# One encoder layer on one core: the launch, with its loads, first rounding and products on zeros in another order

## The chip, the cores and the metric

The kernel runs on 1 core of one Trainium2 chip. A core has five engines that run side by side, each with its own queue of instructions: TensorE (PE, matrix products, with its weight loads shown as PEld), VectorE (DVE), ScalarE (ACT), GpSimd (POOL) and SyncE (SP, which here only issues DMAs). The metric is the device time of one execution in microseconds (us). The median of 3 runs of the kernel before is 2184.84 us (2183.32 to 2185.92).

## What is computed

The reference is one encoder layer on x of 512 tokens by 2048 features, in float32:

```python
h = rmsnorm(x, attn_norm_w[l])
proj = h @ w_in[l]
...
attn = mixture_of_dilations(_heads(aq, ATTN_HEADS), _heads(ak, ATTN_HEADS),
                            _heads(av, ATTN_HEADS), rel_bias_table)
...
mixed = jnp.concatenate([attn_out, gla_out], axis=-1) @ w_out[l]
x = x + mixed

h = rmsnorm(x, ffn_norm_w[l])
x = x + (jax.nn.silu(h @ w_gate[l]) * (h @ w_up[l])) @ w_down[l]
...
return rmsnorm(x, final_norm_w)
```

Only the first two lines matter for this change: the launch prepares h, and the first products compute the columns of proj that hold the attention values.

## The kernel before

**Products.** TensorE multiplies in a rounded float type (fp32r). To keep float32 accuracy, every operand is held as two tiles: hi, the value rounded to fp32r, and lo, the rest (value minus hi). A product is then three matmuls that add into one PSUM bank: hi by hi, hi by lo, lo by hi. In run_job these are lines 346 to 348, in the order x-hi by weight-hi, x-hi by weight-lo, x-lo by weight-hi.

**Weights.** The class Stream (object st) loads weights in pieces of 512 KB (two k blocks of 128 rows by 512 columns). A piece has two halves, and half n is the weights of loop step n of a job. load() issues the DMAs on SP while fewer than st.limit pieces are held. split(upto) rounds halves up to that number: ACT casts hi (L237), and rests() has DVE subtract to get lo (L218).

**x.** xt holds x as loaded, tokens on partitions. prep(k) makes feature block k of h: four transposes on TensorE against the identity tile idn (L450) put the block into a PSUM bank; ACT scales it by the norm weight column wcol into hi (L455); for k < 2 DVE computes lo straight from PSUM (L457), and ACT then writes the unrounded block into fB (L458); for k of 2 and more DVE takes lo from that unrounded block (L460). ACT and DVE take turns on one PSUM bank. Each pair of blocks q (2q and 2q+1) is followed by sums_x(q), a generator of three steps: sums of quarter blocks on DVE, then two steps that round them (L154 on ACT, L145 on DVE). It waits in the deque side, and run_side lets it advance by about one step at the end of each loop step.

**The launch.** The kernel begins with a memset of the tile warm to zero, then idn is loaded on SP's queue and wrow1 (the norm weights) on ACT's. start0, which the first job calls, makes five products of warm by warm (spin(5), two instructions each), then issues on SP, alternately, four x blocks of 256 KB (first_x, L423) and four weight blocks of 256 KB (L1127): x block 0, weight half 0, x block 1, weight half 1 and so on, and after them the rest of x, two further weight pieces and small tensors. It then transposes wrow1 into wcol, calls prep(0), makes three products on zeros and rounds the first weight half.

**The first job.** job_av(0) has 16 loop steps, one for each k. In step i four banks b = 0 to 3 get three matmuls each. The function between0(i, b), called ahead of bank b, places the next blocks of h: prep(1) ahead of bank 2 of step 0, prep(2) and prep(3) in step 1, and prep(i+2) ahead of bank 2 of each later step. before0(i) adds the sums of squares on ACT (L498) from step 3 on. The second weight half is rounded at the start of step 1.

**Order.** The program is scheduled by hand: each engine executes its instructions in the order of the Python code, and waits on semaphores for what it reads or overwrites. Slots hands out tile buffers first in, first out.

Of the kernel before, what the change touches and what calls it, by code (L numbers as in the profile page):

```python
# [19 lines left out]
OP = mybir.AluOpType  # L20
# [92 lines left out]
def put(*slots):  # L113
    for s in slots:
        if s.home is not None:
            s.home.free.append(s.i)


def layer(nc, tc, x, attn_norm_w, w_in, rel_table, gw_f, gb_f, gw_b, gb_b, gla_norm_w, w_out,
# [3 lines left out]
    w_gate, w_up, w_down, out = w_gate[0], w_up[0], w_down[0], out[0]  # L123
    pe, act, dve, pool, sp = nc.tensor, nc.scalar, nc.vector, nc.gpsimd, nc.sync
    mm = pe.matmul

    with tc.manual_schedule(), \
# [6 lines left out]
        s4 = Slots(p4, N4, 1024, "b")  # L134
# [24 lines left out]
        idn = cst.tile([P, P], F32, name="idn")  # L159
# [83 lines left out]
        st = Stream()  # L243
        AHEAD = 3
# [16 lines left out]
        side = deque()  # L261
# [46 lines left out]
        def run_job(j):  # L308
            if j.start:
                j.start()  # L310
            if j.limit:
                st.limit = j.limit
            banks = j.banks or [ps.get() for _ in range(4)]
            per = len(j.kts) // j.n
            for i in range(j.n):
                if j.before and j.tail is None:
                    j.before(i)
                st.load()
                st.split(j.first + i + (min(AHEAD, i + 1) if j.between else j.lead(i)) +
                         (0 if j.tail is None else max(0, 4 * (4 * j.tail + i - 3) // 3)))  # L320
                if j.tail is not None:
                    j.before(i)
                st.lag = j.fine
                st.rests(j.first + i + 1)
                _, _, wh, wl = st.halves[j.first + i]
                ks = j.kts[i * per:(i + 1) * per]
                for b in range(4):
                    if j.between:
                        j.between(i, b)
                    for s_, k in enumerate(ks):  # L330
                        xh, xl = j.acts(k)
                        first = i == 0 and s_ == 0
                        last = i == j.n - 1 and s_ == per - 1
                        if j.kind == "A":
                            o = banks[b].t
                            c = slice(b * P, (b + 1) * P)
                            mm(o, wh.t[:, c], xh.t, start=first, stop=False)  # L337
                            mm(o, wh.t[:, c], xl.t, start=False, stop=False)  # L338
                            mm(o, wl.t[:, c], xh.t, start=False, stop=last)  # L339
                        else:  # L340
                            n = 512 // per
                            o = banks[b].t[:, 0:n]
                            c = slice(b * P, (b + 1) * P)
                            w = slice(s_ * n, (s_ + 1) * n)
                            on = bool(j.banks)
                            mm(o, xh.t[:, c], wh.t[:, w], start=first and not on, stop=False, skip_group_check=on)  # L346
                            mm(o, xh.t[:, c], wl.t[:, w], start=False, stop=False, skip_group_check=on)  # L347
                            mm(o, xl.t[:, c], wh.t[:, w], start=False, stop=last, skip_group_check=on)  # L348
                    if j.fine and b < 3:
                        state["credit"] += j.rate / 4  # L350
                        if state["credit"] >= 1:
                            state["credit"] -= 1
                            run_side(1)
                put(wh, wl)
                if j.drop:
                    for k in ks:
                        j.drop(k)
                state["ahead"] += j.ahead
                while state["ahead"] >= 1:
                    state["ahead"] -= 1  # L360
                    next(state["sums"], None)
                if i < j.n - 1:
                    state["credit"] += j.rate / 4 if j.fine else j.rate
                    n = int(state["credit"])
                    state["credit"] -= n
                    run_side(n)
            j.evac(banks)
# [62 lines left out]

        dve.memset(warm, 0.0)
        xt[0] = [s4.get(F32, [P, 4, 256]) for _ in range(2)]
        sp.dma_start(out=idn, in_=c_idn)
        act.dma_start(out=wrow1, in_=attn_norm_w[0].rearrange("(r c) -> r c", c=P))

        rb = {}
        hT = {}
# [6 lines left out]
        def prep(k):  # L444

            w = wcol[:, W_ATT + k:W_ATT + k + 1]
            q, odd = divmod(k, 2)
            b = ps.get()
            for t in range(4):
                pe.transpose(b.t[:, t * P:(t + 1) * P], x_block(k, t), idn)  # L450
            hi, lo = hT[k] = s4.pair()
            if not odd:
                fB[q] = s4.get(F32, [P, 2, 512])
            f = fB[q].t[:, odd]
            act.activation(hi.t, b.t, AF.Copy, scale=w)  # L455
            if k < 2:
                dve.scalar_tensor_tensor(lo.t, b.t, w, hi.f, op0=OP.mult, op1=OP.subtract)  # L457
            act.activation(f, b.t, AF.Copy, scale=w)  # L458
            if k >= 2:
                dve.tensor_tensor(lo.t, f, hi.f, op=OP.subtract)  # L460
            put(b)
            if odd:
                side.append(sums_x(q))

        def block_sums(f, t13, t24):

# [7 lines left out]
        def sums_x(q):  # L474

            a, z = slice(0, 256), slice(256, 512)
            f = fB.pop(q)
            t_ = s4.get(F32, [P, 2, 512])
            t13, t24 = t_.t[:, 0], t_.t[:, 1]
            block_sums(f.t, t13, t24)  # L480
            put(f)
            yield
            x_ = {}
            slots, (x_["T2"], x_["T4"]) = side_by_side(t24, KEEP_X)
            yield
            more, (x_["T1"], x_["T3"]) = side_by_side(t13, KEEP_X)
            put(t_)
            for name, k, h in (("B11", 2 * q, a), ("B21", 2 * q + 1, a), ("B22", 2 * q + 1, z)):
                x_[name] = hT[k][0].whole[:, :, h]
            xi[q] = dict(x_, slots=slots + more)  # L490
            yield
# [617 lines left out]
        def spin(n):  # L1109

            b = ps.get()
            for _ in range(n):
                mm(b.t[:, 0:P], warm, warm, start=True, stop=True)
            put(b)

        def start0():
            tables(EXP_LN)
            spin(5)
            for k in range(4):
                first_x(k)  # L1120
                if k % 2 == 0:
                    pc = st.pieces[k // 2]
                    pc[1] = s4.get()
                    st.held += 1
                    st.n_dma += 1
                for src, dst in pc[0]:
                    sp.dma_start(out=dst(pc[1].t)[:, k % 2:k % 2 + 1], in_=src[:, k % 2:k % 2 + 1])  # L1127
            for c in range(1, 4):
                xt[c] = [s2.get() for _ in range(4)]
            load_x(1, 0, 256)  # L1130
            st.limit = 3
            st.load()
            load_x(1, 256, 512)
            st.limit = 4
            st.load()
            load_x(2, 0, 512)
            load_x(3, 0, 512)
            for r, w in ((0, ffn_norm_w), (16, gla_norm_w), (24, gb_f), (28, gb_b)):
                n = w[0].shape[0] // P
                sp.dma_start(out=wrow2[r:r + n], in_=w[0].rearrange("(r c) -> r c", c=P))  # L1140
            bias_loads(sp)
            b = ps.get(F32, [P, 16])
            pe.transpose(b.t, wrow1, idn[0:16, 0:16])
            dve.tensor_copy(wcol[:, 0:16], b.t)
            put(b)
            prep(0)
            spin(3)
            st.split(1)

        def between0(i, b):  # L1150
            if i == 0 and b == 2:
                prep(1)
            if i == 1 and b in (1, 3):
                prep(2 + b // 2)
            if i > 1 and b == 2 and i + 2 < KT:
                prep(i + 2)
# [179 lines left out]
        for c in range(4):  # L1336
            j = job("B", [piece512(w_out, c * 512, k) for k in range(0, KT, 2)], list(range(KT)),
                    lambda k: mixh[k], evac_out(c), rate=1.0, start=start_out(c), before=before_out(c), limit=3)
# [654 lines left out]
        for c in range(4):  # L1993
            j = job("B", [piece512(w_down, c * 512, k) for k in (0, 2)], list(range(4)),
                    lambda k: gT[k], evac_down(c), before=before_down(c))
# [153 lines left out]
```

## Time and profile before

| what | value |
|---|---|
| median of 3 runs | 2184.84 us |
| the profiled execution, span | 2184.5 us |
| PE busy | 2163.5 us |
| DVE busy | 1770.9 us |
| ACT busy | 1195.3 us |
| PE busy in the first 17 us | 12.74 us |
| PE busy from 17 to 100 us | 83.00 us |

The times are from one profiled execution. In a line of the order of time the first number is the start in us, the second the duration; then come engine, source line, operation, output tile, input tiles, shapes, and in square brackets the idle time just before and what ended it. "b" and "a" are the two families of buffers (4 KB and 2 KB for each partition), "ps" a PSUM bank. SPq and ACTq are DMAs issued on the queue of that engine. In a line of waits, the first engine and line waited for the second: total us, times, longest us. Matmuls are pipelined, so the start of the next one tells more than the duration of one.

### The profile page before, as it was taken

How to read it: one execution, taken by the hardware profiler on the slowest of the kernel's cores; microseconds unless marked ns; L12 is line 12 of the kernel's file. 1: busy time of each engine (PE TensorE's matmuls, PEld its weight loads, DVE VectorE, ACT ScalarE, POOL GpSimd, SP SyncE). 2: the span in 40 equal slices, each digit the busy share in tenths (PEclk: the TensorE clock that was granted, in tenths of full speed). 3: DMA queues.
4: the chain of work that ended last, by engine and by line, in shares of the span. 5: the costliest groups of instructions: out<-in, count | busy, mean ns of one | idle time of the engine just before them, and what ended most of it. 6: DMA issues, size and time to landing. Idle time of an engine off the chain costs nothing.

```text
span 2184.5 us, 34570 instructions
## 1 busy us (share of the span) xinstructions
PE 2163.5 (99%) x12618; PEld 1904.8 (87%) x12618; DVE 1770.9 (81%) x3072; ACT 1195.3 (55%) x2190; POOL 338.8 (16%) x474
## 2 busy tenths in 40 slices
PE   9999999999999999999999999999999999999998
PEld 7888778888888888988888888888888899999986
DVE  5699867776677557899999899998999888898885
ACT  7454456776654335555555555555555655555562
POOL 0012231110101110012212122121221220021300
PEclk9999999999999999999999999999999999999999
DMA  6367784543337873377767777767776975576982
GB/s 191 125 182 176 184 240 131 179 142 105 116 97 255 293 261 107 116 186 176 194 174 184 184 176 193 176 183 184 176 194 176 264 195 181 184 182 157 283 305 78
DMA packets 256856, 397.81 MB, mean 182 GB/s; under 512 B 18925, under 2 KB 154269, under 8 KB 256686
## 3 DMA queue, kind: packets, MB, share of 16 engines
q1 hardware_dynamic: 201406, 272.49, 39.1%
q0 software_dynamic: 54960, 122.58, 24.9%
q8 instruction: 99, 1.62, 0.3%
q14 instruction: 71, 0.58, 0.1%
q10 hardware_dynamic: 320, 0.53, 0.1%
HBM read 285.37 MB, written 64.29 MB: 160 GB/s over the span
## 4 chain that ended last, share of the span: by engine, by line
PE 87%; issue 6%; DMA 3%; DVE 2%; ACT 1%; POOL 0%; DVEq 0%; ACTq 0%; SPq 0%; POOLq 0%
PE ps L1494 26%; PE ps L1480 13%; PE ps L346 6%; PE ps L347 6%; PE ps L348 6%; PE ps L1850 5%; PE ps L1851 5%; PE ps L1849 5%; DMA b<-a 3%; PE ps L339 3%; PE ps L337 3%; PE ps L338 3%; PE ps L651 1%; PE ps L1075 1%; PE ps L619 1%
## 5 line engine op out<-in xcount | busy, mean ns | idle before, releaser
L1398 ACT CAST b<-b 128x768 fp32r<-128x768 f32 (+1 forms) x537 | 489.2, 945 | 337.4 <-DVE b L1403 150.0
L1403 DVE TENSOR_TENSOR b<-b,b 128x768 fp32r<-128x768 f32 (+1 forms) x537 | 564.0, 1084 | 33.9 <-ACT b L1398 21.9
L1494 PE MATMUL ps<-b,b 128*128 128x512 f32 x1552 | 451.2, 393 | 0.4 <-ACT b L1398 0.2
L1494 PE MATMUL ps<-a,b 128*128 128x512 f32 x1248 | 366.0, 394 | 3.3 <-DVE b L1514 3.3
L1494 PEld LDWEIGHTS ps<-b,b 128*128 128x128 f32 x1552 | 263.6, 189 | 30.6 <-ACT b L1398 0.7
L1480 PEld LDWEIGHTS ps<-b,b 128*128 128x128 f32 x1552 | 252.9, 190 | 36.0
L1480 PE MATMUL ps<-b,b 128*128 128x256 f32 x1552 | 275.9, 281 | 0.0
L1480 PEld LDWEIGHTS ps<-a,b 128*128 128x128 f32 x1248 | 208.0, 189 | 34.1 <-DVE b L1403 0.4
L1494 PEld LDWEIGHTS ps<-a,b 128*128 128x128 f32 x1248 | 207.3, 189 | 23.4 <-ACT a L1526 4.0
L1480 PE MATMUL ps<-a,b 128*128 128x256 f32 x1248 | 223.9, 281 | 0.0
L1385 DVE TENSOR_TENSOR b<-b 128x512 f32<-128x512 f32 x244 | 167.4, 686 | 20.1 <-DMA b<-in_w_down_dram 6.7
L1850 PE MATMUL ps<-b,b 128*128 128x256 f32 x624 | 176.9, 284 | 0.0
L1851 PE MATMUL ps<-b,b 128*128 128x256 f32 x624 | 176.9, 284 | 0.0
L1849 PE MATMUL ps<-b,b 128*128 128x256 f32 x624 | 176.9, 284 | 0.0
L346 PE MATMUL ps<-b,b 128*128 128x512 f32 x352 | 140.7, 400 | 2.0 <-ACT b L237 2.0
L347 PE MATMUL ps<-b,b 128*128 128x512 f32 x352 | 138.4, 393 | 0.9 <-DVE b L218 0.9
L348 PE MATMUL ps<-b,b 128*128 128x512 f32 x352 | 138.2, 392 | 0.0
L1851 PEld LDWEIGHTS ps<-b,b 128*128 128x128 f32 x624 | 119.9, 192 | 0.0
L1849 PEld LDWEIGHTS ps<-b,b 128*128 128x128 f32 x624 | 119.9, 192 | 0.0
L1850 PEld LDWEIGHTS ps<-b,b 128*128 128x128 f32 x624 | 119.9, 192 | 0.0
L218 DVE TENSOR_TENSOR b<-b,b 128x512 fp32r<-128x512 f32 x144 | 96.5, 687 | 24.0 <-ACT b L237 23.9
L1387 DVE TENSOR_TENSOR b<-b,b 128x256 f32<-128x256 f32 x244 | 103.8, 426 | 8.4
(294 smaller groups left out, 4352.2 us busy)
## 6 DMA issues: line engine op xcount, KB each, us to landing
b<-in_w_gate_dram SPq DMA_DIRECT2D x109, 512.0 KB, 4.1
b<-in_w_up_dram SPq DMA_DIRECT2D x88, 512.0 KB, 3.8
b<-in_w_down_dram SPq DMA_DIRECT2D x88, 512.0 KB, 6.6
b<-in_w_in_dram SPq DMA_DIRECT2D x78, 512.0 KB, 4.2
b<-a POOLq DMA_DIRECT2D x150, 256.0 KB, 4.5
b<-in_w_out_dram SPq DMA_DIRECT2D x32, 512.0 KB, 6.6
gd<-b POOLq DMA_DIRECT2D x22, 512.0 KB, 3.9
b<-gd SPq DMA_DIRECT2D x22, 512.0 KB, 5.7
```

Source lines behind the costliest of these rows:

```text
L346: mm(o, xh.t[:, c], wh.t[:, w], start=first and not on, stop=False, skip_group_check=on)
L347: mm(o, xh.t[:, c], wl.t[:, w], start=False, stop=False, skip_group_check=on)
L348: mm(o, xl.t[:, c], wh.t[:, w], start=False, stop=last, skip_group_check=on)
L1385: dve.tensor_tensor(s_[:, :, 0:2], r[:, :, 1:3], r[:, :, 0:1].to_broadcast(shape), op=OP.add)
L1387: dve.tensor_tensor(s_[:, :, 3], s_[:, :, 2], r[:, :, 3], op=OP.add)
L1398: act.copy(o, src)
L1403: dve.tensor_tensor(o, src, h, op=OP.subtract)
L1480: mm(o, wl, xh, start=False, stop=end, skip_group_check=True)
L1494: mm(o.rearrange("p (s t) -> p s t", s=2), wh, x_, start=first and p == 0, stop=False, skip_group_check=True)
L1849: mm(o, xh[:, t], wh, start=first and h == 0, stop=False, skip_group_check=True)
L1850: mm(o, xh[:, t], wl, start=False, stop=False, skip_group_check=True)
L1851: mm(o, xl[:, t], wh, start=False, stop=last, skip_group_check=True)
```

## The change

idn's load moves from SP's queue to ACT's, behind wrow1, so that the x block comes first on SP. In start0 the three products on zeros after prep(0) become two ahead of it and one after it, and the rounding of the first weight half moves from there into prep(0): a new function first_half does it on DVE (a copy for hi and a subtraction for lo), between ACT's hi of x block 0 and DVE's lo of it. In between0, the second weight half is rounded and x block 1 prepared ahead of bank 1 of step 0 (they were placed at the start of step 1 and ahead of bank 2 of step 0). sums_x(0), which was queued when block 1 was prepared, is queued at the front of side in step 2. The condition in run_job is rewritten with it.

```diff
@@ run_job
-                st.split(j.first + i + (min(AHEAD, i + 1) if j.between else j.lead(i)) +
+                st.split(j.first + i + (min(AHEAD, i + 1) if j.between and i else 1 if j.between else j.lead(i)) +
                          (0 if j.tail is None else max(0, 4 * (4 * j.tail + i - 3) // 3)))
@@ layer
-        sp.dma_start(out=idn, in_=c_idn)
         act.dma_start(out=wrow1, in_=attn_norm_w[0].rearrange("(r c) -> r c", c=P))
+        act.dma_start(out=idn, in_=c_idn)
@@ prep
             act.activation(hi.t, b.t, AF.Copy, scale=w)
+            if k == 0:
+                first_half()
             if k < 2:
                 dve.scalar_tensor_tensor(lo.t, b.t, w, hi.f, op0=OP.mult, op1=OP.subtract)
...
-            if odd:
+            if odd and q:
                 side.append(sums_x(q))
+
+        def first_half():
+
+            h = st.halves[0]
+            r = st.pieces[0][1].t[:, 0:512]
+            h[2], h[3] = s4.pair()
+            dve.tensor_copy(h[2].t, r)
+            dve.tensor_tensor(h[3].t, r, h[2].f, op=OP.subtract)
+            st.n_conv = 1
@@ start0
+            spin(2)
             prep(0)
-            spin(3)
-            st.split(1)
+            spin(1)
@@ between0
-            if i == 0 and b == 2:
+            if i == 0 and b == 1:
+                st.split(2)
                 prep(1)
+            if i == 2 and b == 0:
+                side.appendleft(sums_x(0))
```

## The prediction

> **What bounds the kernel now.** I read the page's shares first, then the busy time by stretch, TensorE's own waits, and at last the order of time in the launch.
>
> ```profile
> span 2184.5 us, 34570 instructions
> PE 2163.5 (99%) x12618; PEld 1904.8 (87%) x12618; DVE 1770.9 (81%) x3072; ACT 1195.3 (55%) x2190; POOL 338.8 (16%) x474
> ...
> 0.00:17.00 17.00, 12.74 (x42) 9.78 (x43) 5.26 (x11) 5.56 (x8) 0.20 (x4) 1.00 0.87 274
> 17.00:100.00 83.00, 83.00 (x393) 67.45 (x392) 57.58 (x121) 59.28 (x139) 2.79 (x5) 1.00 0.47 152
> ...
> PE ps L346 <- ACT b L237: 2.0, 2, 1.5
> ...
> PE ps L347 <- DVE b L218: 0.9, 1, 0.9
> PE ps L450 <- DMA b<-in_x_dram: 0.4, 1, 0.4
> ```
>
> TensorE (PE) bounds it: idle for 21.0 of 2184.5 us. The stretches (columns: length, then PE, PEld, DVE, ACT, POOL busy, clock, DMA share, GB/s) show 4.26 us of that idle time before 17 us and none from 17 to 100. The waits say what the launch waits for: a first weight half being rounded (L237, L218), and x. Whatever PE gains before 17 us is a gain of everything that follows, if later stages can keep up.
>
> ```profile
> 0.74 0.42 ACTq L434 DMA_DIRECT2D wrow<-in_attn_norm_w_dram  x1
> 0.74 0.38 SPq L433 DMA_DIRECT2D idn<-in_c_idn_dram  x1
> ...
> 1.18 0.42 SPq L423 DMA_DIRECT2D b<-in_x_dram  x1
> ...
> 1.65 0.50 SPq L1127 DMA_DIRECT2D b<-in_w_in_dram  x1
> 2.19 0.43 SPq L423 DMA_DIRECT2D b<-in_x_dram  x1
> ...
> 3.49 0.28 PE L1143 MATMUL ps<-idn,wrow 16*128 16x16 f32 x1
> ...
> 4.13 1.12 PE L450 MATMUL ps<-idn,b 128*128 128x128 f32 x4 [0.35 <-DMA b<-in_x_dram]
> ...
> 5.04 1.49 PE L1113 MATMUL ps<-warm 128*128 128x128 f32 x6
> ...
> 5.28 0.69 ACT L455 ACTIVATE b<-ps,wcol 128x512 fp32r<-128x512 f32 x1 [2.81 <-PE ps L450]
> 6.00 0.75 DVE L457 SCALAR_TENSOR_TENSOR b<-ps,wcol,b 128x512 fp32r<-128x512 f32 x1 [2.02 <-ACT b L455]
> 6.79 0.69 ACT L458 ACTIVATE b<-ps,wcol 128x512 f32<-128x512 f32 x1 [0.82 <-DVE b L457]
> 7.38 0.61 ACT L237 CAST b<-b 128x512 fp32r<-128x512 f32 x1
> 8.02 0.69 DVE L218 TENSOR_TENSOR b<-b,b 128x512 fp32r<-128x512 f32 x1 [1.26 <-ACT b L237]
> ...
> 8.04 0.79 PE L346 MATMUL ps<-b,b 128*128 128x512 f32 x1 [1.51 <-ACT b L237]
> ...
> 10.21 0.63 PE L347 MATMUL ps<-b,b 128*128 128x512 f32 x1
> ...
> 10.63 0.63 PE L348 MATMUL ps<-b,b 128*128 128x512 f32 x1
> ...
> 11.06 1.05 PE L450 MATMUL ps<-idn,b 128*128 128x128 f32 x4
> ...
> 13.62 0.57 PE L347 MATMUL ps<-b,b 128*128 128x512 f32 x1
> ...
> 14.24 1.13 ACT L237 CAST b<-b 128x512 fp32r<-128x512 f32 x2
> ...
> 14.91 0.49 PE L346 MATMUL ps<-b,b 128*128 128x512 f32 x1 [0.48 <-ACT b L237]
> ...
> 16.26 0.50 PE L347 MATMUL ps<-b,b 128*128 128x512 f32 x1 [0.86 <-DVE b L218]
> ...
> 17.51 0.40 PE L347 MATMUL ps<-b,b 128*128 128x512 f32 x1
> ...
> 17.74 0.40 PE L348 MATMUL ps<-b,b 128*128 128x512 f32 x1
> ```
>
> One chain: x lands (4.1), is transposed, rounded by ACT (L455), its rest taken by DVE (L457), scaled again by ACT (L458, which waits for L457), and only then does ACT round the first weights (L237). The first real product starts at 8.04 though its x operand was ready at 5.97. The second weight half is rounded behind the whole second x tile (14.24), so PE waits at 14.91 and at 16.26; after 16.26 it is not idle again in this stage. I call the product at 16.26 number 14 and measure by it. Products start 0.42 to 0.43 us apart at first (10.21, 10.63), 0.23 apart later (17.51, 17.74); the change comes at 13.6, 5.6 us after 8.04, while the clock column reads 1.00 throughout, so the spacing must be read, not that column.
>
> **Edits with no cost.** The new condition in run_job gives 1 at step 0, as min(AHEAD, 1) did, and the old value elsewhere. The eight products on zeros stay eight (5+3 becomes 5+2+1). One ACT cast becomes one DVE copy. Weight loads are freed at the same loop steps, since a limit of 3 on held pieces stands in both.
>
> **DMAs.** On SP the first x block moves from 1.18 to 0.74 and all that follows by 0.44 (first weights 1.21, second x block 1.75, second weights, one issue of 0.5 later, about 2.23). idn goes to ACT's queue behind wrow, so at about 1.18; the table load behind it ends near 2.9, long before ACT's first work.
>
> ```profile
> DMA to landing us min/median/max: 1.9/1.9/1.9
> DMA to landing us min/median/max: 3.7/3.7/3.7
> DMA to landing us min/median/max: 4.5/5.4/6.2
> 1.18 2.90 DMA b<-in_x_dram
> ```
>
> In order: wrow (8 KB), the first weight block, the later x blocks (256 KB each), the first x block. idn's own landing is not shown. Its bounds are 1.9 (wrow) and 3.7 (weights, behind other traffic): 3.1 to 4.9. PE is busy with zeros until about 3.5 anyway, so 3.1 costs nothing, 4.9 costs 1.4. At 64 KB it is nearest the small one; I take 2.5, landing 3.7, a delay of 0.2. x lands at 3.64 and is hidden.
>
> **First product.** wrow's transpose at 3.69, its 0.28, then four of the zero instructions at 1.49/6 = 0.25 each, so x's transposes start at 4.97, 0.84 later than now. This is a cost of the change. ACT's L455 follows 0.84 late too, 6.12 to 6.81. DVE meanwhile has the first weights (issued 1.21, plus 3.7: 4.91). Its copy is not in the trace: 0.18 (the 128x16 copy, L1144) to 0.75 (L457); I take 0.6, as ACT's cast of that shape is, then L218's 0.69: done by 6.2, so hidden under ACT's 6.81. If the weights take 4.5 as the second x block, L457 and all behind it on DVE, and ACT's L458, slip by 0.2. The first product waits for 6.81 only and starts at 6.85: 1.19 earlier. Its third needs L457's rest at 7.59 and would start at 7.71.
>
> ```profile
> 3.81 0.17 DVE L1144 COPY wcol<-ps 128x16 f32<-128x16 f32 x1 [2.81 <-PE ps L1143]
> ```
>
> **Second weights.** After three products (6.85 + 3 x 0.43 = 8.14) come the second x tile's transposes (four at 0.22, to 9.0; that x block landed by 1.75 + 4.5 = 6.25). ACT: L458 to 8.3; the second half's cast to 8.9 (its block, issued 2.23, lands by 6.7 to 8.4); L455 9.1 to 9.8; DVE's rest to 10.6. PE has nine products left, to 9.0 + 9 x 0.43 = 12.9. All operands are there 2.3 us early: both waits (0.48 and 0.86) go. Nothing takes their place: the third tile's block lands well before its transposes at about 13.3.
>
> **Sum.** Number 14 starts at 12.9 + 0.43 = 13.3. If half-rate spacing again lasts 5.6 us from the first product, it ends at 12.45, and the last 0.85 us shrinks by 0.4: 12.9. Against 16.26 that is -3.35. Span 2184.5 - 3.35 = 2181.15. The profiled span lies 0.34 below the runs' median of 2184.84, so I forecast 2181.5 for the median.
>
> **Is it kept?** ACT is the cover that is thinnest.
>
> ```profile
> 30.00:40.00 10.00, 10.00 (x52) 8.27 (x51) 6.59 (x14) 10.00 (x26) 0.00 (x0) 1.00 0.26 86
> ...
> 38.13 0.69 DVE L460 TENSOR_TENSOR b<-b,b 128x512 fp32r<-128x512 f32 x1 [0.47 <-ACT b L458]
> ...
> 39.43 0.39 PE L348 MATMUL ps<-b,b 128*128 128x512 f32 x1
> ...
> 20.45 0.71 ACT L154 CAST a<-b 128x256 fp32r<-128x256 f32 x2
> ```
>
> From 30 to 40 us ACT has no idle time, and tile 8's rest is ready at 38.82 for a product at 39.43: 0.6 us of slack. If PE moves 3.35 earlier and ACT did not, PE would stall about 2.7. But ACT starts earlier with PE, and sums_x(0), now queued at step 2, moves its two L154 casts (0.6 us of ACT each) from steps 1 and 2 to 3 and 4, behind ACT's early rush. By tile 8 ACT has three of these casts behind it instead of four, so its lead grows by 0.6; for tile 9 the count is equal. I charge nothing. With less lead the cost is bounded by that 2.7.
>
> **Rivals.**
>
> Half rate ends sooner. PE would be idle only about 0.7 us between 3.5 and the first product (0.2 for idn, 0.5 behind the last zeros), against 1.86 now (0.35 and 1.51). Release at 10.2 instead of 12.45 saves another 2.2 x (1 - 0.23/0.43) = 1.0; release before 6.85 would be limited by the operands of the second step (L457 to 7.6, then L458, the cast, L455 to 9.6 and the rest at 10.4), so number 14 at about 10.6, -5.65. So -4.4 to -5.6, about 2180.0. For it: fewer gaps. Against: today's 2.5 us of zeros and 1.49 more released nothing by 10. The Trainium skill, "TensorE: Matmul & The Clock Gate", Part 1, says that the array runs at half rate until one window of about 3.4 us was busy, and that the window runs freely, so that the cold stretch differs between runs of one kernel. The halved spacing agrees; by that rule the stretch would last 3.4 to 6.8 us from steady work, an estimate, and either rival time can show in one run.
>
> idn is late. At 3.7 us from issue the first product would be at 8.05 as now; only the waits of the second step go, and the total is -3.35 + 1.2, about 2182.7. Against: it is a quarter of the weights' size. For: it shares the engines with x.
>
> ACT gives it back. Between none and 2.7 of 3.35 lost at tiles 8 and 9: about 2183.2.
>
> Slower. From 157 to 250 us the chain runs through accumulating transfers, and PE's largest later wait is there.
>
> ```profile
> PE ps L1494 <- DVE b L1514: 3.5, 5, 1.8
> ```
>
> Five such waits cost 3.5, the longest 1.8. Shifted side work changes which slots the tiles get. If three more units fall into the longest wait, +5.4 - 3.35 = +2.1, 2186.9; it decides from two such waits on. Against: after 64 us ACT and DVE follow PE with idle time, and all issues move together.
>
> The change doesn't do what it says: more zeros are not issued, only earlier ones; with the weights' rounding off ACT's chain that does not touch the sum.
>
> **How the numbers follow.** Forecast 0.50 (own range 2180.6 to 2182.4), sooner full rate 0.24, late idn 0.10, ACT gives back 0.10, slower 0.06. A measurement here tells about 0.2%, 4.4 us, from no change. Beyond that on the fast side lie most of the second case and the forecast's edge: 0.25. On the slow side half of the last case: 0.04. Within: 0.71. The range leaves out the fastest of the second case and the last: 2179.4 to 2184.0.
>
> **What would show it.** Right: first product near 6.9, waiting for ACT L455 and no more for L237; no PE wait at the second step; number 14 near 12.9; no PE wait from there to 60; the later stages the same by length. Wrong: x's transposes after 5.5 (late idn), spacing 0.23 before 11 (sooner), PE waits for L460 or L455 between 25 and 45 (ACT), more or longer waits at L1494 (slower).

## The result, and the profile after

The changed kernel takes 2182.02 us (median of 21 runs) against 2185.53 for the kernel before (21 runs): a ratio of 0.9984, 95% interval 0.9978 to 0.9991. The profiled execution has a span of 2179.8 us, 4.7 below the one before. These are the stretches (length, then PE, PEld, DVE, ACT, POOL busy, clock, DMA share, GB/s) and TensorE's waits in the changed kernel's first 20 us.

```profile
0.00:17.00 17.00, 14.31 (x62) 12.07 (x63) 5.20 (x10) 7.86 (x12) 0.20 (x4) 1.00 0.90 282
17.00:100.00 83.00, 83.00 (x389) 67.03 (x388) 58.16 (x124) 57.07 (x135) 2.79 (x5) 1.00 0.46 150
...
PE ps L1154 <- DMA idn<-in_c_idn_dram: 1.3, 1, 1.3
PE ps L1124 <- DVE warm L431: 1.1, 1, 1.1
PE ps L346 <- ACT b L455: 0.3, 1, 0.3
```

TensorE's idle time before 17 us fell from 4.26 to 2.69 us, and from 17 to 100 there is still none. The waits for the weight rounding (L237, L218) are gone, and the first product waits only for x's rounding (L455). A wait is new: 1.3 us for idn. The order of time of the same kernel shows where it stands.

```profile
1.23 0.51 ACTq L434 DMA_DIRECT2D idn<-in_c_idn_dram  x1
...
4.84 0.26 PE L1154 MATMUL ps<-idn,wrow 16*128 16x16 f32 x1 [1.28 <-DMA idn<-in_c_idn_dram]
...
5.23 0.42 DVE L472 CAST b<-b 128x512 fp32r<-128x512 f32 x1
...
5.68 0.69 DVE L473 TENSOR_TENSOR b<-b,b 128x512 fp32r<-128x512 f32 x1
...
7.15 0.69 ACT L455 ACTIVATE b<-ps,wcol 128x512 fp32r<-128x512 f32 x1 [4.10 <-PE ps L450]
...
7.88 0.80 PE L346 MATMUL ps<-b,b 128*128 128x512 f32 x1 [0.35 <-ACT b L455]
...
10.47 0.39 PE L347 MATMUL ps<-b,b 128*128 128x512 f32 x1
...
10.69 0.39 PE L348 MATMUL ps<-b,b 128*128 128x512 f32 x1
...
12.53 0.39 PE L347 MATMUL ps<-b,b 128*128 128x512 f32 x1
```

idn lands 3.6 us after its issue. DVE's rounding of the first weights (L472, L473) is done at 6.37, before ACT's L455 starts, and so is hidden. The first product starts at 7.88, only 0.16 earlier than before, but from 10.47 on products start 0.23 us apart instead of 0.43, nothing waits at the second step, and product 14 starts at 12.53 instead of 16.26: 3.73 us earlier. The transposes of the later x blocks show that the gain is kept (before, then after; the last two times are the first and the last start): the last one starts 3.5 us earlier.

```profile
L450 PE MATMUL ps<-idn,a x48: 270/273/273, 21.2 to 59.8; 128*128 128x128 f32 x48
L450 PE MATMUL ps<-idn,a x48: 270/272/274, 17.3 to 56.3; 128*128 128x128 f32 x48
```

The rest of the 4.7 has another source, seen in the waits of before around 1775 us:

```profile
PE ps L1850 <- DVE b L1403: 0.9, 1, 0.9
```

The profile of the changed kernel has no such wait, and one of the versions below that is faster still has it again (e9, 0.94 us). It is scatter between executions; with the waits around 190 to 250 us, which also differ from profile to profile, it makes single spans uncertain by about a microsecond. Product 14 is therefore the better gauge of the launch.

### The profile page after: what moved, and what is told of

Its sections match the earlier page's. It is cut to its first block, busy times and chain, and to the rows that moved or that the text cites. A ratio compares the mean times of both kernels' runs of the same rounds, so it can differ in the third digit from the quotient of the medians.

```text
span 2179.8 us, 34563 instructions
## 1 busy us (share of the span) xinstructions
PE 2161.3 (99%) x12618; PEld 1904.2 (87%) x12618; DVE 1771.2 (81%) x3073; ACT 1195.9 (55%) x2189; POOL 338.9 (16%) x474
## 4 chain that ended last, share of the span: by engine, by line
PE 89%; issue 6%; DMA 2%; DVE 2%; ACT 1%; POOL 0%; ACTq 0%; DVEq 0%; POOLq 0%
PE ps L1508 27%; PE ps L1494 14%; PE ps L346 6%; PE ps L347 6%; PE ps L348 6%; PE ps L1864 5%; PE ps L1865 5%; PE ps L1863 5%; PE ps L339 3%; PE ps L337 3%; PE ps L338 3%; DMA b<-a 2%; PE ps L662 1%; PE ps L1086 1%; PE ps L630 1%
## 5 line engine op out<-in xcount | busy, mean ns | idle before, releaser
L218 DVE TENSOR_TENSOR b<-b,b 128x512 fp32r<-128x512 f32 x143 | 95.9, 686 | 26.1 <-ACT b L237 26.0
```

## The experiments

All twelve at a glance. "Full rate" is the time from which TensorE's products, zeros or transposes follow each other at half the first spacing, read from the starts in each profile to about 0.2 us; the ratio is to runs of the kernel before on the same chip.

| kernel | first product | full rate | product 14 | median | ratio (95% interval) |
|---|---|---|---|---|---|
| before | 8.04 | 14.0 | 16.26 | 2185.53 | |
| changed | 7.88 | 10.4 | 12.53 | 2182.02 | 0.9984 (0.9978 to 0.9991) |
| e0, changed again | 8.16 | 12.1 | 13.51 | 2181.81 | 0.9982 (0.9973 to 0.9991) |
| e1, idn on SP | 6.11 | 4.7 | 10.06 | 2178.84 | 0.9966 (0.9953 to 0.9978) |
| e9, the same again | 6.56 | 6.0 | 10.44 | 2179.34 | 0.9972 (0.9963 to 0.9981) |
| e2, idn ahead of wrow | 7.74 | 8.7 | 11.72 | 2182.24 | 0.9982 (0.9973 to 0.9990) |
| e3, three zeros out | 7.11 | 12.9 | 13.31 | 2183.24 | 0.9991 (0.9982 to 1.0000) |
| e4, ACT rounds first weights | 10.27 | 13.8 | 15.60 | 2185.73 | 1.0000 (0.9991 to 1.0009) |
| e5, second weights as before | 7.87 | 11.2 | 15.05 | 2185.29 | 0.9993 (0.9984 to 1.0002) |
| e6, DMA edits alone on before | 9.25 | 15.3 | 17.47 | 2186.97 | 1.0004 (0.9995 to 1.0013) |
| e7, sums as before | 8.05 | 10.0 | 12.53 | 2181.17 | 0.9976 (0.9965 to 0.9986) |
| e8, e1 without three zeros | 6.23 | 12.3 | 12.55 | 2181.77 | 0.9984 (0.9975 to 0.9993) |
| e10, changed, eight first zeros | 6.99 | 5.2 | 10.87 | 2179.64 | 0.9975 (0.9965 to 0.9985) |
| e11, before, more zeros | 8.14 | 6.3 | 14.88 | 2185.72 | 0.9999 (0.9990 to 1.0008) |

e0, e1, e3 and e5 ran on one chip, e2, e4, e6 and e7 on a second, e8 to e11 on a third. The kernel before had medians of 2185.77, 2186.26 and 2185.07 there, so medians from different chips are compared to about a microsecond at best.

### Is the early full rate the change's, or chance? (e0)

The changed kernel, unaltered.

> The changed kernel, profiled a second time. In the first profile idn landed only at 4.84 us, the first product started at 7.88 and the spacing of the products fell from 0.43 to 0.23 us at about 10.4. Theory A (the zeros and the shorter gaps bring the full rate sooner): the spacing falls at 10 to 10.7 again and product 14 starts at 12.5 again. Theory B (the moment of full rate is a matter of chance between executions): it falls anywhere up to about 14, and product 14 moves with it up to 14.2. In both the time is about 2182, ratio 0.998 to 0.999.

Neither extreme. In the order of time of this second profile the spacing is still 0.43 from 11.31 to 11.74 and 0.23 only from 12.12:

```profile
5.12 0.26 PE L1154 MATMUL ps<-idn,wrow 16*128 16x16 f32 x1 [1.56 <-DMA idn<-in_c_idn_dram]
...
11.31 0.63 PE L348 MATMUL ps<-b,b 128*128 128x512 f32 x1
11.74 0.54 PE L346 MATMUL ps<-b,b 128*128 128x512 f32 x1
12.12 0.39 PE L347 MATMUL ps<-b,b 128*128 128x512 f32 x1
12.35 0.39 PE L348 MATMUL ps<-b,b 128*128 128x512 f32 x1
```

So the moment moves by about 1.7 us between two executions of one kernel, and product 14 with it by 1.0. Differences of product 14 between single profiles have to be larger than that to count.

### What the new place of idn costs (e1, e9, e6, e2)

e1, and the same kernel again as e9:

```diff
         act.dma_start(out=wrow1, in_=attn_norm_w[0].rearrange("(r c) -> r c", c=P))
-        act.dma_start(out=idn, in_=c_idn)
+        sp.dma_start(out=idn, in_=c_idn)
```

(with the SP line ahead of the ACT one, as before the change)

> idn's load back on SP ahead of x, the rest as changed. If the wait for idn is a cost of its new place, it is gone: x transposes at 4.8 after two products on zeros, first product at about 6.7 instead of 7.88. If the moment of full rate follows the start of steady work, product 14 gains the whole 1.2 (11.4); if that moment stays at about 10.4, half-rate products fill the time and product 14 starts at 12.3, a gain of 0.2 to 0.3 only. Time 0.2 to 1.2 us below the changed kernel's.

> The version with idn back on SP and all else as changed, profiled and timed a second time. The first profile had no wait for idn, the products close together from 4.7 us on and product 14 at 10.06. If full rate follows unbroken work from the first zeros, it comes between 4.5 and 8 us again and product 14 starts at 10.0 to 10.9. If it was luck, full rate comes after 8 and product 14 at 11 to 12.3. Time 2178 to 2180, 6 to 7 us below before: faster than both kernels.

Order of time of e1:

```profile
3.49 0.28 PE L1154 MATMUL ps<-idn,wrow 16*128 16x16 f32 x1
...
4.72 0.61 PE L450 MATMUL ps<-idn,b 128*128 128x128 f32 x4
...
6.11 0.50 PE L346 MATMUL ps<-b,b 128*128 128x512 f32 x1 [0.55 <-ACT b L455]
...
6.45 0.40 PE L347 MATMUL ps<-b,b 128*128 128x512 f32 x1
...
10.06 0.39 PE L347 MATMUL ps<-b,b 128*128 128x512 f32 x1
```

The wait for idn is gone, and four transposes take 0.61 us in place of 1.06: full rate has come before the first product. It was expected to gain at most 1.2; product 14 gained 2.5 (and 2.1 in e9 against the changed kernel's first profile). The times agree: 2.5 to 3.2 us below the changed kernel's. On the one chip where both ran, every run of e1 (2178.20 to 2179.41) is below every run of e0 (2180.38 to 2183.57). This version beats both kernels. The DMA edits are thus the one part of the change that costs.

e6 is the kernel before with those two DMA edits alone:

> The kernel before with only the two DMA edits: x first on SP, idn behind wrow on ACT's queue. If the late idn costs what the changed kernel's trace shows, PE waits 1.3 to 1.5 us for it, x's transposes start at 5.1 instead of 4.13 and the first product at 9.0; product 14 at 17.0 to 17.3; time 0.7 to 1.0 us above before, ratio 1.0003 to 1.0005. If x's earlier load pays for it, both stay.

The first product starts at 9.25 and product 14 at 17.47, both 1.2 later than before, a little more than expected; the time's interval reaches to both sides of 1. In e2 the two loads on ACT's queue change places:

```diff
-        act.dma_start(out=wrow1, in_=attn_norm_w[0].rearrange("(r c) -> r c", c=P))
         act.dma_start(out=idn, in_=c_idn)
+        act.dma_start(out=wrow1, in_=attn_norm_w[0].rearrange("(r c) -> r c", c=P))
```

> The changed kernel with the two loads on ACT's queue exchanged: idn first, wrow behind it. Theory Q (idn is late because its 64 KB share the engines with SP's x and weights, whenever it is issued): it still takes about 3.6 us, lands near 4.3, the first product starts at 7.4 and PE still has a gap of 0.8 us behind the first zeros; time about 0.5 us below the changed kernel's. Theory I (it was late because it was issued second): it lands by 3.5, there is no gap, the first product starts near 6.2 and the full rate comes before 6, as with idn on SP; time about 2179. If wrow is the late one now, PE waits for it instead, to at least 3.7.

The third of these came true. Order of time of e2; below it the landing of idn in e2 and of wrow in the changed kernel, each issued first on ACT's queue, at 0.74:

```profile
0.74 0.45 ACTq L433 DMA_DIRECT2D idn<-in_c_idn_dram  x1
0.74 0.43 SPq L423 DMA_DIRECT2D b<-in_x_dram  x1
...
1.22 0.53 ACTq L434 DMA_DIRECT2D wrow<-in_attn_norm_w_dram  x1
...
4.70 0.25 PE L1154 MATMUL ps<-idn,wrow 16*128 16x16 f32 x1 [1.13 <-DMA wrow<-in_attn_norm_w_dram]
...
DMA to landing us min/median/max: 3.1/3.1/3.1
DMA to landing us min/median/max: 2.4/2.4/2.4
```

Now the 8 KB of wrow take 3.5 us, where they took 1.9 in the kernel before. Size alone does not make a load late, then: in the second place 8 KB take 3.5 us and 64 KB 3.6 to 4.0; in the first place, beside x's block, 8 KB take 2.4 and 64 KB 3.1. The place is worth about 1 us to wrow and 0.5 to idn, the size 0.7 in the first place and less in the second. But the second place is at once behind SP's first 256 KB block and behind another load of ACT's own queue. Which of the two counts, and whether the engines, the memory or the queues make the load wait, was not tried.

### Zeros and the half rate (e3, e8, e10, e11)

e3 takes the three zeros around the first x tile out of the changed kernel:

```diff
-            spin(2)
             prep(0)
-            spin(1)
```

> The changed kernel without the two and the one products on zeros around the first x tile; the first five stay. The x transposes follow idn at once: first product at about 7.0. If the zeros bring the full rate sooner (A), it now comes at 13.5 or later and product 14 starts at 13.4, 0.9 us later than in the changed kernel, time up by 0.9. If the zeros do nothing for the rate (B), it falls at about 10.4 and product 14 starts at about 12.0, time down by 0.5.

e8 makes the same edit with idn on SP:

> idn on SP as in the version before this one, but without the two and the one products on zeros. PE then has gaps of 0.4 us ahead of x's transposes and of about 1 us behind them. If these three zeros keep PE's work unbroken and that is what brings the full rate, it comes only 3.4 us or more after the first product at about 6.2, product 14 starts at 11.5 to 12.5 and the time is 1.5 to 2.5 us above that of the version with them. If the first five zeros are enough, product 14 starts near 10 and the time is the same.

e8 went as the first theory has it. The first product is about as early as in e1 and e9, but half rate lasts to 12.3, product 14 starts 2.1 to 2.5 later than in those two, and the median is 2.4 above that of e9, on the same chip. Order of time of e8:

```profile
11.95 0.55 PE L348 MATMUL ps<-b,b 128*128 128x512 f32 x1
12.33 0.39 PE L346 MATMUL ps<-b,b 128*128 128x512 f32 x1
12.55 0.39 PE L347 MATMUL ps<-b,b 128*128 128x512 f32 x1
```

e3 points the same way but shows less. Its first product starts 0.77 earlier than in the changed kernel, half rate lasts to 12.9 (13.5 or later was expected), product 14 starts at 13.31 and the median is 1.2 higher; but e0, which has the three zeros, has its product 14 at 13.51, and the runs of the two overlap. The other way round, e10 fills the wait for idn:

```diff
-            spin(5)
+            spin(8)
```

> The changed kernel with eight products on zeros at the start instead of five: PE works through the 1.3 to 1.6 us in which it waits for idn. The first product stays at about 8.0. If the gap is what delays the full rate, this comes by 8 us and product 14 starts at 11.6 to 11.9 instead of 12.5 to 13.5, time 0.7 to 1.7 us below the changed kernel's. If the gap does not matter for the rate, product 14 stays at 12.5 to 13.7.

Order of time of e10:

```profile
1.06 3.78 PE L1124 MATMUL ps<-warm 128*128 128x128 f32 x16 [1.06 <-DVE warm L431]
...
4.77 0.28 PE L1154 MATMUL ps<-idn,wrow 16*128 16x16 f32 x1
...
5.62 0.60 PE L450 MATMUL ps<-idn,b 128*128 128x128 f32 x4
...
6.99 0.50 PE L346 MATMUL ps<-b,b 128*128 128x512 f32 x1 [0.55 <-ACT b L455]
...
10.87 0.39 PE L347 MATMUL ps<-b,b 128*128 128x512 f32 x1
```

The first use of idn is as late as ever (4.77), yet the transposes run at full rate and the first product starts 0.9 earlier than in the changed kernel, where the same start was expected: at full rate the second lot of zeros and the transposes are shorter too. Product 14 gains 1.7, and the time lies near e1's. So much of what the late idn costs is not the wait itself but what the gap does to the rate: late without a gap, product 14 is at 10.87, against 10.06 and 10.44 with idn early and 12.53 and 13.51 with the gap. Last, e11 gives the kernel before more zeros and nothing else:

```diff
+            spin(1)
             prep(0)
-            spin(3)
+            spin(6)
```

> The kernel before with more products on zeros alone: one ahead of the first x tile, six instead of three behind it, so that PE has hardly a gap up to the first product. If unbroken work brings the full rate, it comes between 4.5 and 8 us, the transposes of the second x tile start at about 9.9 instead of 11.06, and product 14, which ACT's and DVE's chain behind them sets, at about 14.9 instead of 16.26: time 1.2 to 1.5 us below before. If the zeros do nothing, the rate changes at 11 to 14 and product 14 starts at 16.2.

Order of time of e11:

```profile
8.14 0.49 PE L346 MATMUL ps<-b,b 128*128 128x512 f32 x1 [0.94 <-ACT b L237]
...
9.21 0.39 PE L348 MATMUL ps<-b,b 128*128 128x512 f32 x1
9.44 0.40 PE L346 MATMUL ps<-b,b 128*128 128x512 f32 x1
...
13.53 0.50 PE L346 MATMUL ps<-b,b 128*128 128x512 f32 x1 [1.42 <-ACT b L237]
...
14.88 0.49 PE L347 MATMUL ps<-b,b 128*128 128x512 f32 x1 [0.85 <-DVE b L218]
```

The first products are 0.23 apart, and product 14 is at 14.88 as expected; the waits of the second step remain, and the one for L237 grows to 1.42 because TensorE arrives sooner at the same late cast. Behind these gaps the products are still 0.23 us apart: once full rate has come, a gap of 1.42 does not take it back. The time shows no gain: its interval (about 2 us to either side) is too wide for one of 1.4.

### The two places where the weights are rounded (e4, e5)

e4 gives the first rounding back to ACT, behind its work on x:

```diff
-            if k == 0:
-                first_half()
...
             spin(2)
             prep(0)
             spin(1)
+            st.split(1)
```

> The changed kernel with the first weight half rounded by ACT again, behind its work on the first x tile. If this rounding was on the path, the first product starts at 9.9 instead of 7.9 (ACT's second scaling ends at 9.3, then 0.6 for the cast) and product 14 about 2 us later; time 1.5 to 2.5 us above the changed kernel's, so almost all of the gain gone. If it was hidden (the late idn being what counts), the first product moves by less than 0.5.

It loses the whole gain, and more than the 1.5 to 2.5 us expected: the ratio to before is 1.0000. The first product starts 2.4 later; in the order of time of e4 it waits for L237, which stands behind ACT's second scaling:

```profile
9.03 0.69 ACT L458 ACTIVATE b<-ps,wcol 128x512 f32<-128x512 f32 x1 [0.82 <-DVE b L457]
9.61 1.12 ACT L237 CAST b<-b 128x512 fp32r<-128x512 f32 x2
...
10.27 0.80 PE L346 MATMUL ps<-b,b 128*128 128x512 f32 x1 [2.36 <-ACT b L237]
```

That is 0.4 later than expected, because idn landed at 5.22 in this execution. The gap of 2.36 us also puts off the full rate, to 13.8. e5 puts the second half and the second tile back:

```diff
-            if i == 0 and b == 1:
-                st.split(2)
+            if i == 0 and b == 2:
                 prep(1)
```

> Only the placing of the second weight half and of the second x tile undone. If these two waits of the second step are what the changed kernel saves there, they return: the second half is rounded behind the second x tile at about 13.3, its rest is ready near 14.5, and product 14 starts at 14.5 instead of 12.5, PE waiting for L237 and L218. Time 2.0 us above the changed kernel's (ratio to before about 0.9993). If they were not on the path, product 14 stays at 12.5.

Order of time of e5:

```profile
14.32 0.51 PE L346 MATMUL ps<-b,b 128*128 128x512 f32 x1 [1.42 <-ACT b L237]
15.05 0.50 PE L347 MATMUL ps<-b,b 128*128 128x512 f32 x1 [0.22 <-DVE b L218]
```

The waits come back, 1.42 for L237 and 0.22 for L218, product 14 starts at 15.05, and most of the gain is lost (median 3.3 above the changed kernel's; 2.0 expected). Both placings are needed: each alone leaves another wait of the chain standing.

### The sums of the first pair (e7)

```diff
-            if odd and q:
+            if odd:
...
-            if i == 2 and b == 0:
-                side.appendleft(sums_x(0))
```

> The changed kernel with the sums of the first two blocks queued where they were before. If ACT's lead is what this move protects, the casts of the sums stand in ACT's queue 0.6 us ahead of tile 8 again and PE shows waits for L462 or L455 between 20 and 45 us, up to 0.6 us in all. If the lead is enough without it, PE has no wait there and the time is that of the changed kernel within 0.5 us.

TensorE shows no wait from 17 to 100 us, product 14 stands at 12.53 as in the changed kernel, and the time is not told apart (its median is 0.85 lower, from another chip). ACT's lead is enough without this move.

## Why the prediction was right

The forecast was 2181.5, a gain of 3.35; measured are 2182.02 and a gain of 3.5. The mechanism stood at its two main places, and two terms of the sum were mis-sized in opposite directions, so that the closeness of the number is luck.

**Right.** The first product waits for x's rounding and no longer for the weights' (e4: without that, 2.4 us later). The second step's two waits go and nothing takes their place (e5: they return). DVE's copy took 0.42 where 0.6 was taken, and its work ended at 6.37, before L455 began at 7.15. That cover is not always there: in e8, with idn early and no zeros around the first x tile, the first product waits 0.78 us, and what ends the wait is DVE's L473. The new condition changed nothing visible, and the zeros stayed at eight. TensorE had no wait to 100 us, so the launch's gain was kept; the allowance for ACT's lead was not needed, and e7 shows that the sums' move did not matter for it.

**Mis-sized: idn.** I put its landing 2.5 us after issue, because 64 KB seemed nearest to wrow's 8 KB. It took 3.6 to 4.0, at the upper bound that the weights' row gave. So the rival "idn is late" came true in its own terms: the first product at 7.88, where 8.05 was worked out, not at 6.85. e2 shows why the choice was bad: wrow's 1.9 us were those of the first place on its queue, and in the second place even wrow takes 3.5.

**Mis-sized: the half rate.** I let it last 5.6 us from the first product, as I read it in the kernel before, to 12.45. That reading was short. In the kernel before, the product behind the one at 13.62 starts 0.41 later:

```profile
14.03 0.39 PE L348 MATMUL ps<-b,b 128*128 128x512 f32 x1
```

So half rate lasted to about 14.0 there, 6.0 us. In the changed kernel it ended at 10.4 in one profile and 12.1 in the other, 2.5 and 3.9 us from the first product. The rival "half rate ends sooner" came true as well. My sum had 13.3 - 6.85 = 6.45 us of half-rate work from the first product to product 14; from 7.88 that gives 14.33, and the measured 12.53 is 1.8 less, where I had allowed 0.4. The first product is 1.0 later and the full rate saves 1.4 more: 12.53 against the forecast 12.9. In the second profile the same two errors are 1.3 and 0.7, and product 14 stands at 13.51. The failing step was to count from the first product: the zeros ahead of it count too, and what starts the count anew is a gap.

In every one of the fourteen profiles full rate comes 3.5 to 7.0 us after TensorE takes up work behind its last gap of 0.78 us or more before that moment: from 1.06 where there is no such gap (to 4.7 in e1, 6.0 in e9, 5.2 in e10, 6.3 in e11), from the end of the wait for idn or wrow where that is the last one (4.84 to 10.4, 5.12 to 12.1 in e0, 4.70 to 8.7 in e2, 4.83 to 11.2 in e5, 5.02 to 10.0 in e7), and from the first product where a longer gap lies ahead of it (8.04 to 14.0 before, 7.11 to 12.9 in e3, 10.27 to 13.8 in e4, 9.25 to 15.3 in e6, 6.23 to 12.3 in e8). Gaps of 0.35 start nothing anew. This rule was fitted to the profiles after they were seen, and where between 0.35 and 0.78 us its limit lies is open. Transposes at least do not act as a gap: in e9 and e11 four of them take 0.86 us, and full rate comes 0.4 and 1.2 us behind them. The Trainium skill, "TensorE: Matmul & The Clock Gate", Part 1, gives one busy window of about 3.4 us that runs freely, hence 3.4 to 6.8 as an estimate from it. The fourteen profiles agree within the error of the reading (e0, the longest, is 0.2 above); that the phase of such a window makes the spread is the page's account, and no run here sets it.

**Overlooked.** These two terms are one. A late idn was priced as a shift of 1.2 us; it also makes a gap of 1.3 to 1.6 us after 2.5 us of zeros, which throws away the progress to full rate. e1 and e10, which remove the gap in two ways, gain 1.7 to 2.5 at product 14 and about 2.2 to 3.2 in the median (by the ratios to before on the chip of each, 1.5 to 3.9).

## What to carry to other kernels

At a launch, keep TensorE's stream without gaps from its first instruction until full rate has come: here a wait of a microsecond ahead of that moment cost itself and then half of the rate for several more. A small load that everything needs goes ahead of the big blocks in the order of issue; here another queue did not bring it past them. And when an edit list mixes several moves, undo them one at a time: here the two roundings carried the gain, the zeros were worth 2.4 us with idn early (e8 against e9), the sums' move did nothing that could be measured, and the DMA edits cost 2.5 to 3.2 us.

## What was not expected of the hardware

The place of a load in the order of issue moved its landing at least as much as its size did: the 8 KB of wrow landed in 1.9 us when issued at 0.74 beside idn (before), in 2.4 beside x's 256 KB (changed kernel), and in 3.5 when issued at 1.22 behind both (e2). The clock column reads 1.00 through all of the half-rate stretch, so only the spacing of the products shows it. And products of zeros bring the full rate as products of data do: in e10 and e11 it came before any product of data, at 5.2 and 6.3 us. A gap counts for more before that moment than after it: behind a gap of 0.78 us full rate took another 5.8 and 6.1 us to come (e3, e8), while a gap of 1.42 us after it had come left it standing (e5, e11).
